# Seven block products in place of eight in six channel groups of a spatial-gating stage, with the values normalized early

## The chip, the cores and the metric

The kernel runs on one core of a Trainium2 chip. A core has five engines that the text names: TensorE (PE) for matrix products, with its weight loads (PEld) shown apart, VectorE (DVE), ScalarE (ACT), GpSimd (POOL) and SyncE (SP), which only issues transfers. Each engine works through its own instructions in order and waits on semaphores for the others. SP and ACT issue the transfers between the chip's memory and the core; sixteen DMA engines carry them. The metric is the device time of one execution in microseconds (us), the median over runs.

## The reference, cut to what matters

One inference step of a two-layer trunk, for 1024 prompt tokens and 64 sample tokens (8 sequences of 8), together 1088 rows of width 1024, in float32. The change touches the even layer:

```python
z = rms_norm(x, norm_g) @ w_in
zq, zk, zv, ga, zu, zvb, gb = split(z)
o_a = rms_norm(diff_attention(q, k, v)) * (1 - lam_init) * silu(ga)
u = gelu(zu)
vb = layer_norm(gelu(zvb), ln_g, ln_b)      # vb of the sample tokens is an output
mixed = chunk_spatial(vb, sp_w, sp_b)       # per group g of 128 channels: w_g (lower triangle, 128x128) times each chunk of 128 tokens, plus sp_b
o_b = u * mixed * silu(gb)
y = x + concat(o_a, o_b) @ w_out
```

`chunk_spatial` works on eight channel groups. For the sample tokens a past of 512 tokens comes from a paged cache of keys and values.

## The kernel before, in words

Tokens stand in columns, in three chunks: 0 and 1 of 384, 2 of 320 (`CH`). The normalized input is held transposed in eight pieces k of 128 channels, split in two numbers: `xh[n]` is its value rounded to a format that PE takes in one pass, `xl[n]` the rest. Weights are split alike (`load_w`): a raw tile arrives by SP, ACT rounds it (hi), DVE or POOL takes the difference (lo). A dense product (`mm3`) is then three matmuls per piece k: hi by `xh`, hi by `xl`, lo by `xh`; eight pieces make 24 matmuls into one PSUM tile.

The stages around the change, in time: attention of the prompt tokens; then the sample attention, which reads 32 pages of keys and 32 of values (`pages`, `vpages`), transposes each key page on PE (`ktp`) and lets ACT copy it back (`kT`, L537); then the spatial stage; then the output projection (`yo`). The sample attention has little work for PE between its waits, so a list `fill` puts other work between its steps, one item after another: first the rest of the gates (`gate_a`: product ga, ACT, DVE, then POOL multiplies the attention rows that ACT has loaded back from `oT_d` as `oTr`, and ACT stores them), then 36 units of value projection (`vb_unit`, product zv, four column blocks by nine row tiles), which store to `vb_d`. `NPRE` gates of 24 stand already in the attention before.

The spatial stage runs over 24 units (group g, chunk n). `b_dense` makes zu and gb, gelu on ACT, the gate by a tanh on ACT, a product on DVE (L743) and one on POOL (u, L744). `b_mix` follows `ML` units later: for each 128 tokens one full float32 matmul of the normalized values by the group's weights (mx, L755), the bias added on DVE (mxs), the product with u on DVE (ob, L766), and a store to `oT_d`. In the first five units `vb_norm` loads the nine row tiles of `vb_d`, gelu on ACT, statistics on DVE, the reciprocal root on POOL (lrv), and two scalings on DVE (L720, L721); `mix_setup` masks and transposes the mixing weights.

Names in tiles carry the group, chunk or piece. Who comes first on an engine is decided when the program is built: instructions go out in the order of a list scheduler, which may interleave neighbouring pieces of the code, and semaphores keep what depends on what.

## Time and profile before

| what | value |
|---|---|
| median of 3 runs | 1791.06 us (1790.74 to 1792.69) |
| profiled execution, its own time | 1789.87 us |
| its span, first to last instruction | 1788.1 us |
| mean granted clock of PE | 0.991 |
| PE busy | 1742.9 us, 97% |
| DVE, ACT, POOL busy | 56%, 42%, 34% |
| spatial stage in the span | 817.9 to about 1028 us |

Times in rows are microseconds of the span, or ns where a mean is given. A timeline row has the start, the length, the engine, the line, the operation and what it writes and reads; "xN" joins N instructions, and a bracket at the end is idle time before it with the one that ended it. A window row gives for each engine the busy time in that stretch.

### The profile page before, as it was taken

To read this page: it belongs to the slowest core of one execution; us is meant where nothing else is said; L and a number is where in the kernel's file an instruction comes from. 1 tells how busy PE (TensorE), PEld (TensorE's weight loads), DVE (VectorE), ACT (ScalarE), POOL (GpSimd) and SP (SyncE) were. 2 spreads that over 40 slices of the span, in tenths; PEclk is the share of its full clock that TensorE was granted. 3 is DMA by queue.
4 is the path that set the end of the run, shared out by engine and by line. 5 is a ranking of instruction groups with operands and counts; after the bars stand their busy time and mean duration, and the time that the engine had idled before them with its cause. 6 is when DMAs were issued, how large, how long until landed. Compare 5 with 4: busy or idle time off the path is not lost.

```text
span 1788.1 us, 31862 instructions
## 1 busy us (share of the span) xinstructions
PE 1742.9 (97%) x11437; PEld 1631.3 (91%) x11437; DVE 1006.3 (56%) x2231; ACT 754.5 (42%) x1934; POOL 605.6 (34%) x881
## 2 busy tenths in 40 slices
PE   8999999999999999999999999999899999998998
PEld 8898999999999888889999999999899999996777
DVE  6988988888892322324833442534265445667442
ACT  5666666665763222223222332423252334345241
POOL 5656655565653221011522100144012223235240
PEclk8999999999999999999999999999999999998999
DMA  7202211220223766747221362433134334438741
GB/s 212 59 20 75 68 42 45 68 67 19 67 71 121 244 218 216 242 142 221 72 77 60 109 188 74 134 94 92 59 121 144 101 119 125 129 116 264 239 127 71
DMA packets 223141, 211.55 MB, mean 118 GB/s; under 512 B 22253, under 2 KB 200982, under 8 KB 222982
## 3 DMA queue, kind: packets, MB, share of 16 engines
q1 hardware_dynamic: 203350, 194.29, 35.1%
q10 hardware_dynamic: 19632, 15.21, 2.8%
q8 instruction: 91, 1.49, 0.4%
q14 instruction: 68, 0.56, 0.1%
HBM read 151.29 MB, written 56.24 MB: 116 GB/s over the span
## 4 chain that ended last, share of the span: by engine, by line
PE 66%; DVE 15%; DMA 6%; ACT 5%; POOL 4%; issue 3%; SPq 0%; ACTq 0%; POOLq 0%; DVEq 0%
PE o L1371 5%; PE yo L148 3%; PE yo L150 3%; PE yo L149 3%; PE vg L148 3%; PE vg L149 3%; PE vg L150 3%; PE zv L148 2%; PE zu L148 2%; PE zv L149 2%; PE zv L150 2%; PE zu L150 2%; PE gb L148 2%; PE zu L149 2%; PE gb L149 2%
## 5 line engine op out<-in xcount | busy, mean ns | idle before, releaser
L409 ACT ACTIVATE p<-s,nm 128x256 f32<-128x256 f32 (+7 forms) x128 | 95.0, 747 | 44.5 <-DVE nm L406 26.1
L396 PE MATMUL s<-ks,qs 128*128 128x512 f32 (+3 forms) x384 | 95.6, 363 | 3.9 <-DVE ks L381 2.2
L92 ACT CAST qs<-qs 64x256 fp32r<-64x256 f32 x128 | 51.7, 404 | 83.5 <-DVE qs L378 77.6
L1118 POOL TENSOR_TENSOR e<-e,k 128x256 f32<-128x256 f32 (+1 forms) x50 | 42.2, 850 | 111.6 <-ACT e L1115 97.6
L396 PEld LDWEIGHTS s<-ks,qs 128*128 128x128 f32 x384 | 64.3, 189 | 14.3 <-ACT qs L92 3.8
L431 PE MATMUL o<-v,at 128*128 128x128 f32 x576 | 75.9, 277 | 1.4 <-ACT at L92 1.4
L136 POOL TENSOR_TENSOR s<-s,mhalf 128x4 f32<-128x4 f32 (+1 forms) x72 | 74.5, 1035 | 5.2
L335 POOL TENSOR_TENSOR sq<-qk 128x256 f32<-128x256 f32 (+1 forms) x72 | 47.8, 664 | 83.1 <-ACT qk L92 82.1
L431 PEld LDWEIGHTS o<-v,at 128*128 128x128 f32 x576 | 70.6, 192 | 4.0 <-ACT at L92 2.4
L834 DVE TENSOR_TENSOR yp<-yp,yo 128x384 f32<-128x384 f32 (+1 forms) x48 | 25.4, 530 | 75.6 <-ACT yp L833 41.7
L404 DVE TENSOR_REDUCE nm<-s 128x1 f32<-128x640 f32 (+3 forms) x64 | 65.2, 1019 | 1.1
L744 POOL TENSOR_TENSOR u<-u,th 128x384 f32<-128x384 f32 (+1 forms) x24 | 28.6, 1192 | 99.8 <-DVE th L743 99.3
L402 DVE TENSOR_TENSOR s<-s,tb 128x256 f32<-128x256 f32 (+1 forms) x128 | 52.5, 412 | 8.9 <-PE s L396 5.8
L415 DVE SCALAR_TENSOR_TENSOR p<-p,fac,p 128x128 f32<-128x128 f32 (+3 forms) x64 | 54.7, 854 | 1.6
L1371 PE MATMUL o<-w1h,oh 128*128 128x512 f32 x128 | 53.0, 414 | 1.2 <-ACT oh L1348 1.2
L92 ACT COPY at<-atp 128x512 f32<-128x512 f32 (+2 forms) x96 | 44.6, 480 | 14.7 <-PE atp L424 14.2
L1371 PE MATMUL o<-w1l,oh 128*128 128x512 f32 x128 | 50.8, 397 | 0.0
L1371 PE MATMUL o<-w1h,ol 128*128 128x512 f32 x128 | 50.3, 407 | 0.0
L743 DVE SCALAR_TENSOR_TENSOR th<-th,gb 128x384 f32<-128x384 f32 (+1 forms) x24 | 12.5, 526 | 65.3 <-ACT th L742 65.3
L424 PE MATMUL atp<-cf,p 128*128 128x128 f32 x288 | 46.7, 273 | 1.7 <-DVE p L415 1.4
L340 POOL TENSOR_TENSOR qk<-qk,s 128x256 f32<-128x256 f32 (+1 forms) x72 | 46.0, 638 | 4.5
L1115 ACT ACTIVATE e<-e 128x512 f32<-128x512 f32 (+1 forms) x50 | 31.1, 623 | 37.4 <-DVE e L1114 33.6
(819 smaller groups left out, 6344.2 us busy)
## 6 DMA issues: line engine op xcount, KB each, us to landing
kp<-in_cache_k SPq DMA_DIRECT2D x32, 512.0 KB
vp<-in_cache_v SPq DMA_DIRECT2D x32, 512.0 KB
or<-oT_d SPq DMA_DIRECT2D x16, 384.0 KB
vb_d<-zs SPq DMA_DIRECT2D x36, 128.0 KB
oT_d<-ob SPq DMA_DIRECT2D x8, 544.0 KB
gt<-g_d SPq DMA_DIRECT2D x34, 128.0 KB
xt<-in_x_prompt SPq DMA_DIRECT2D x8, 512.0 KB
out<-v ACTq DMA_DIRECT2D x64, 64.0 KB
```

The costliest lines, as they stand in the source:

```text
L92: act.activation(o, i_, AF.Copy, scale=scale) if scale is not None else act.copy(o, i_)
L136: pool.tensor_tensor(dst, dst, mhalf[:dst.shape[0], :n], ALU.pow)
L148: pe.matmul(out, lh, rh, start=(s == 0), stop=False)
L149: pe.matmul(out, lh, rl, start=False, stop=False)
L150: pe.matmul(out, ll, rh, start=False, stop=(s == n - 1))
L396: pe.matmul(sc[c][:, k0:k0 + w], qs[:, c, l], kts[h, j][:, c, :w], start=(l == 0), stop=(l == 1))
L402: dve.tensor_tensor(sc[c][:, lo:n], sc[c][:, lo:n], backwards(tb[:, h, 0:n - lo]), ALU.add)
L404: dve.tensor_reduce(nm[:, c:c + 1], sc[c][:, :n], axis=AX.X, op=ALU.max, negate=True)
L409: act.activation(pc[:, :n], sc[c][:, :n], AF.Exp, bias=nm[:, c:c + 1], accum_out=ss[:, c:c + 1])
L415: dve.scalar_tensor_tensor(pt[0][:, :n], pt[1][:, :n], fac, pt[0][:, :n], ALU.mult, ALU.add)
L431: pe.matmul(op[:, :P], at[:, j * P:(j + 1) * P], vts[h, j], start=(j == 0), stop=(j == i))
L1371: pe.matmul(it.mp[:r], lh[:, k, :r], rh[k][:, cs], start=(k == 0 and a == 0), stop=(k == KT - 1 and a == 2))
```

## The change

In groups 2 to 7 (`NCV` = 2) the two projections of chunks 0 and 1 are read as a 2 by 2 block problem: two weight column blocks (zu, gb), two halves of the 1024 input channels, two chunks. The eight products of half by chunk become seven products of sums (Winograd's form): p1 to p7, each of 12 matmuls (four pieces, three parts) of 384 columns. Sums of the input (T1, T2, T4 by `tok_sums`, T3 in place over chunk 1 by `tok_last`) are made once, sums of weight blocks for each group (`load_g`), and seven additions from PSUM put the results together (`b_quad`). Chunk 2 keeps its 48 matmuls of 320 columns.

The normalization goes from the spatial stage into the list `fill`, between the last gates; it stores to a new tensor `vbn_d`, and each group loads its 128 columns (`load_vs`). Gain and bias of the layer norm are taken out of it: the gain enters with mxs, the bias is folded into the mixing bias by two matmuls of 512 columns (wsp) and eight DVE instructions. `fill` now has the 36 value units first and the gates last; `NPRE` goes from 8 to 9. Chunks run in the order 1, 0, 2, and mixing follows one group later.

```diff
-NPRE = 8
+NPRE = 9
...
-ML = 5
+ML = 2
+NCV = 2
+NU = 6
...
+            def vb_norm(i):
+                r = rows(i)
+                vt = pb.tile([P, D], F32, tag="vp", name=f"vbn{i}", bufs=6)
+                nc.sync.dma_start(vt[:r], vb_d[i * P:i * P + r, :])
+                if i == NT - 1:
+                    vx = pb.tile([P, D], F32, tag="vp", name="vx", bufs=6)
+                    nc.sync.dma_start(vx[:r], vb_d[T:, :])
+                    dve.tensor_tensor(vt[:r], vt[:r], vx[:r], ALU.add)
+                act.activation(vt[:r], vt[:r], AF.Gelu)
+                bst = pb.tile([P, 2, 6], F32, tag="bst", name=f"bst{i}", bufs=2)
+                mv = pb.tile([P, 2], F32, tag="mv", name=f"mv{i}", bufs=2)
+                rv = pb.tile([P, 1], F32, tag="lrv", name=f"lrv{i}", bufs=2)
+                for q in range(2):
+                    dve.bn_stats(bst[:r, q, :], vt[:r, q * 512:(q + 1) * 512])
+                dve.bn_aggr(mv[:r], bst[:r].rearrange("p a b -> p (a b)"))
+                rsqrt(rv[:r], mv[:r, 1:2], 1, 1.0)
+                dve.tensor_scalar(vt[:r], vt[:r], mv[:r, 0:1], rv[:r], ALU.subtract, ALU.mult)
...
+                nc.sync.dma_start(vbn_d[i * P:i * P + r, :], vt[:r])
...
+            fill = [lambda c=c, i=i: vb_unit(c, i) for c in range(4) for i in range(NT)]
+            for q, (h, n) in enumerate(du[NPRE:]):
+                fill.append(lambda h=h, n=n: gate_a(h, n, gate_tiles))
+                if 1 < q < NT + 2:
+                    fill.append(lambda i=q - 2: vb_norm(i))
...
+                for hh in range(2):
+                    tp = ps2.tile([P, 512], F32, tag="t", name=f"wsp{hh}", bufs=2)
+                    pe.matmul(tp, ones, wT[:, hh * 4:hh * 4 + 4, :], start=True, stop=True)
+                    for g in range(hh * 4, hh * 4 + 4):
+                        dve.scalar_tensor_tensor(sbc[:, g, :], tp[:, g % 4 * P:(g % 4 + 1) * P], lnc[1][:, g:g + 1], sbc[:, g, :],
+                                                 ALU.mult, ALU.add)
...
+            def put_split(t, k, src):
+                act.copy(t[0][:, k, :], src)
+                dve.tensor_tensor(t[1][:, k, :], src, f32(t[0][:, k, :]), ALU.subtract)
+
+            def tok_diff(k, name):
+                a, c = temp(f"{name}a{k}"), temp(f"{name}c{k}")
+                pool.tensor_tensor(a, f32(xl[1][:, k + 4, :]), f32(xl[1][:, k, :]), ALU.subtract)
+                dve.tensor_tensor(c, f32(xh[1][:, k + 4, :]), f32(xh[1][:, k, :]), ALU.subtract)
+                dve.tensor_tensor(c, c, a, ALU.add)
+                return c
+
+            def tok_sums():
+                for m in (1, 2, 4):
+                    tx[m] = [pb.tile([P, 4, XW], F32R, name=f"t{m}{q}") for q in "hl"]
+                for k in range(4):
+                    a, c = temp(f"ta{k}"), temp(f"tc{k}")
+                    pool.tensor_tensor(a, f32(xl[1][:, k, :]), f32(xl[0][:, k, :]), ALU.subtract)
+                    dve.tensor_tensor(c, f32(xh[1][:, k, :]), f32(xh[0][:, k, :]), ALU.subtract)
+                    dve.tensor_tensor(c, c, a, ALU.add)
+                    put_split(tx[1], k, c)
+                    c = tok_diff(k, "td")
+                    dve.tensor_tensor(c, c, f32(xh[0][:, k, :]), ALU.add)
+                    dve.tensor_tensor(c, c, f32(xl[0][:, k, :]), ALU.add)
+                    put_split(tx[2], k, c)
+                    e = temp(f"te{k}")
+                    dve.tensor_tensor(e, f32(xh[0][:, k + 4, :]), c, ALU.subtract)
+                    dve.tensor_tensor(e, e, f32(xl[0][:, k + 4, :]), ALU.add)
+                    put_split(tx[4], k, e)
+
+            def tok_last():
+                tx[3] = xh[1], xl[1]
+                for k in range(4):
+                    put_split(tx[3], k, tok_diff(k, "tf"))
...
+            def load_g(g):
...
+                gs = []
+                for k in range(4):
+                    gt = pb.tile([P, 8, P], F32, tag="G", name=f"G{g}_{k}", bufs=4)
+                    for x in range(2):
+                        nc.sync.dma_start(gt[:, 3 * x:3 * x + 2, :],
+                                          ap_of(w_in0[0], k * P * n + (4 + 2 * x) * D + g * P, [[n, P], [4 * P * n, 2], [1, P]]))
+                    dve.tensor_tensor(gt[:, 6], gt[:, 3], gt[:, 4], ALU.add)
+                    dve.tensor_tensor(gt[:, 5], gt[:, 0], gt[:, 3], ALU.subtract)
+                    dve.tensor_tensor(gt[:, 2], gt[:, 6], gt[:, 0], ALU.subtract)
+                    dve.tensor_tensor(gt[:, 7], gt[:, 1], gt[:, 2], ALU.subtract)
+                    gs.append(gt)
+                blk = Wg_[g] = [[None] * 4 for _ in range(8)]
+                for a, e in ((0, 3), (3, 6), (6, 8)):
+                    for k in range(4):
+                        hi = pw.tile([P, e - a, P], F32R, tag="wh", name=f"gh{g}_{a}_{k}", bufs=9)
+                        lo = pw.tile([P, e - a, P], F32R, tag="wl", name=f"gl{g}_{a}_{k}", bufs=9)
+                        act.copy(hi, gs[k][:, a:e, :])
+                        (pool if a == 3 else dve).tensor_tensor(lo, gs[k][:, a:e, :], f32(hi), ALU.subtract)
+                        for q in range(a, e):
+                            blk[q][k] = hi[:, q - a, :], lo[:, q - a, :]
...
+            def b_quad(g):
...
+                act.copy(pa_, prod("p1_", A11, xb(0, 0)))
+                add(pb_, pa_, prod("p6_", S2, tb_(2)))
+                add(u[0], pa_, prod("p2_", A12, xb(0, 4)))
+                act.activation(u[0], u[0], AF.Gelu)
+                act.activation(u[2][:, :w2], prod("zu2_", A11 + A12, xb(2, 0) + xb(2, 4), w2), AF.Gelu)
+                add(pa_, pb_, prod("p7_", S3, tb_(3)))
+                p5 = prod("p5_", S1, tb_(1))
+                add(pd_, pa_, p5)
+                add(pb_, pb_, p5)
+                bf = prod("gb2_", A21 + A22, xb(2, 0) + xb(2, 4), w2)
+                add(u[1], pb_, prod("p3_", S4, xb(1, 4)))
+                act.activation(u[1], u[1], AF.Gelu)
+                add(pa_, pa_, prod("p4_", A22, tb_(4)))
+                for n, gv in ((2, bf), (1, pd_), (0, pa_)):
+                    th = tile_("th", f"th{n}_", 2)
+                    gated(u[n], g, n, th, gv)
...
+            order = [(g, n) for g in range(NCV) for n in (1, 0, 2)]
+            for s, (g, n) in enumerate(order):
+                us[g, n] = b_dense(g, n)
+                if s == 0:
+                    load_b(1)
+                    tok_sums()
                 if s == 1:
                     mix_setup()
-                for i in range(2 * s, min(2 * s + 2, NT)):
-                    vb_norm(i)
-                n = 0
-                while s >= ML and mi < min(s, len(units)) and n < 2:
-                    b_mix(*units[mi], us.pop(mi))
-                    mi += 1
-                    n += 1
+                if (g, n) == (NCV - 1, 1):
+                    tok_last()
+                    load_g(NCV)
+                if g and n == 1:
+                    load_vs(g)
+                if g:
+                    b_mix(g - 1, n, us.pop((g - 1, n)))
+            for g in range(NCV, KT + 1):
+                if g < KT:
+                    us.update({(g, n): t for n, t in enumerate(b_quad(g))})
+                    load_vs(g)
+                    load_g(g + 1)
+                for n in (1, 0, 2):
+                    b_mix(g - 1, n, us.pop((g - 1, n)))
 
     lY = ctx.enter_context(ExitStack())
     pY = lY.enter_context(tc.tile_pool(name="pY", bufs=1, side="right", reuse_waits="tile"))
```

The order on ACT ahead of the first copy of transposed keys (kT, sample 0), before. `oT_d<-oTr` is a gate's store, `oTr<-oT_d` a gate's load, g the gate's activation.

```order
L550 DMA vn_8379<-vsm 8x1024
L255 DMA oT_d<-oTr_2_7898 128x256
L250 ACTIVATE g_3_0_7932<-ga_0_7930 128x384
L248 DMA oTr_1_8006<-oT_d 128x384
L255 DMA oT_d<-oTr_0_7931 128x384
L250 ACTIVATE g_3_1_8007<-ga_1_8005 128x384
L248 DMA oTr_2_8061<-oT_d 128x256
L537 COPY kT_1_7981<-ktp_0_1_7988 128x4x128
```

And after; zs is the copy of a value unit from PSUM.

```order
L253 ACTIVATE g_2_2_7853<-ga_2_7851 128x320
L94 ACTIVATE oT_7541<-otp_6_7884,sg 128x128
L94 ACTIVATE oT_7541<-otp_7_7887,sg 128x128
L258 DMA oT_d<-oTr_2_7852 128x256
L554 DMA vn_8422<-vsm 8x1024
L251 DMA oTr_0_10273<-oT_d 128x384
L624 COPY zs_1_8014<-zv_1_7989 128x256
L251 DMA oTr_1_10415<-oT_d 128x384
L624 COPY zs_3_8118<-zv_3_8093 128x256
L541 COPY kT_1_8018<-ktp_0_1_8025 128x4x128
```

Two gate stores and two gate loads ahead of kT have become one store and two loads, with copies of value units between the loads and kT.

The order on POOL from the start of the spatial stage, before. lrv is the reciprocal root of the normalization, u the gated product.

```order
L684 AFFINE_SELECT wn<-wn 128x128 x8
L135 TENSOR_SCALAR lrv_11540<-mv_11539 128x1
L136 TENSOR_TENSOR lrv_11540<-lrv_11540,mhalf 128x1
L744 TENSOR_TENSOR u_0_11482<-u_0_11482,th_0_11484 128x384
L135 TENSOR_SCALAR lrv_11552<-mv_11551 128x1
L136 TENSOR_TENSOR lrv_11552<-lrv_11552,mhalf 128x1
L744 TENSOR_TENSOR u_1_11610<-u_1_11610,th_1_11612 128x384
L135 TENSOR_SCALAR lrv_11653<-mv_11652 128x1
L136 TENSOR_TENSOR lrv_11653<-lrv_11653,mhalf 128x1
L744 TENSOR_TENSOR u_2_11723<-u_2_11723,th_2_11725 128x320
```

And after. ta, tda are differences of `xl` for T1 and T2, g2s and oTr the last gate.

```order
L256 COPY g2s<-g_7_2_11430 128x64
L257 TENSOR_TENSOR oTr_2_11429<-oTr_2_11429,g_7_2_11430 128x256
L819 TENSOR_TENSOR ta_11665<-xl_102,xl_101 128x384
L809 TENSOR_TENSOR tda_11672<-xl_102 128x384
L771 TENSOR_TENSOR u_1_11605<-u_1_11605,th_1_11607 128x384
L725 AFFINE_SELECT wn<-wn 128x128 x8
L819 TENSOR_TENSOR ta_11686<-xl_102,xl_101 128x384
L809 TENSOR_TENSOR tda_11693<-xl_102 128x384
L771 TENSOR_TENSOR u_0_11799<-u_0_11799,th_0_11801 128x384
L819 TENSOR_TENSOR ta_11707<-xl_102,xl_101 128x384
L771 TENSOR_TENSOR u_2_11900<-u_2_11900,th_2_11902 128x320
L809 TENSOR_TENSOR tda_11714<-xl_102 128x384
```

The reciprocal roots are gone from here, and differences of 128x384 stand between the u, in the same queue.

The order on SP late in the sample attention, before. kp and vp are pages of keys and values (ISA sets their address), `vb_d<-zs` the store of a value unit.

```order
L525 ISA
L525 DMA vp_2_10537<-in_cache_v 128x1024
L518 ISA
L518 DMA kp_1_10548<-in_cache_k 128x1024
L525 ISA
L525 DMA vp_3_10657<-in_cache_v 128x1024
L518 ISA
L518 DMA kp_2_10668<-in_cache_k 128x1024
L525 ISA
L525 DMA vp_0_10719<-in_cache_v 128x1024
L621 DMA vb_d<-zs_2_10584 128x256
```

And after. vbn is a row tile of values, loaded from `vb_d` and stored normalized to `vbn_d`.

```order
L529 ISA
L529 DMA vp_3_10744<-in_cache_v 128x1024
L634 DMA vbn_10798<-vb_d 128x1024
L522 ISA
L522 DMA kp_2_10755<-in_cache_k 128x1024
L180 DMA wb0r_11510<-in_w_in 128x2x128
L180 DMA wb0r_11516<-in_w_in 128x2x128
L648 DMA vbn_d<-vbn_10661 128x1024
L180 DMA wb0r_11522<-in_w_in 128x2x128
L648 DMA vbn_d<-vbn_10798 128x1024
L529 ISA
L529 DMA vp_0_10823<-in_cache_v 128x1024
```

Loads and stores of 512 KB for the normalization now stand between the pages.

## Rows read from the trace of the kernel before

**Rows 1.** The page, parts 1 and 2: busy time and tenths of PE.
```profile
PE 1742.9 (97%) x11437; PEld 1631.3 (91%) x11437; DVE 1006.3 (56%) x2231; ACT 754.5 (42%) x1934; POOL 605.6 (34%) x881
PE   8999999999999999999999999999899999998998
```

**Rows 2.** Stretches: length, busy PE, PEld, DVE, ACT, POOL, granted clock, DMA share, GB/s.
```profile
580.00:600.00 20.00, 16.33 (x91) 16.01 (x90) 4.55 (x8) 4.21 (x9) 3.89 (x5) 0.83 0.68 218
...
740.00:760.00 20.00, 20.00 (x180) 18.07 (x179) 7.20 (x16) 6.70 (x18) 3.08 (x4) 1.00 0.85 286
...
820.00:840.00 20.00, 20.00 (x125) 19.93 (x124) 8.28 (x24) 8.94 (x17) 2.76 (x10) 1.00 0.92 313
840.00:860.00 20.00, 20.00 (x123) 19.68 (x123) 20.00 (x42) 9.46 (x17) 8.02 (x11) 1.00 0.45 119
860.00:880.00 20.00, 20.00 (x125) 20.00 (x124) 20.00 (x31) 5.46 (x13) 15.91 (x10) 1.00 0.23 65
```

**Rows 3.** Waits of PE from 560 to 1040 us: total, times, longest.
```profile
PE ktp L536 <- ACT kT L537: 3.7, 1, 3.7
PE ktp L536 <- DMA kp<-in_cache_k: 0.7, 1, 0.7
```

**Rows 4.** Timeline of PE, first group of the spatial stage: start, length, instruction.
```profile
817.86 0.34 PE L148 MATMUL zu<-xh,wb0h 128*128 128x384 f32 x1
...
824.05 0.33 PE L148 MATMUL zu<-xh,wb0h 128*128 128x384 f32 x1
...
826.13 0.33 PE L149 MATMUL gb<-xl,wb0h 128*128 128x384 f32 x1
```

**Rows 5.** Timeline of PE: mixing matmuls, and one page's key transposes.
```profile
914.16 0.83 PE L755 MATMUL mx<-wT,vb 128*128 128x128 f32 x6
...
596.01 1.04 PE L536 MATMUL ktp<-cf,kp 128*128 128x128 f32 x8
```

**Rows 6.** Timeline of ACT and its queue around the long wait.
```profile
582.48 0.37 ACTq L255 DMA_DIRECT2D oT_d<-oTr  x1
...
587.98 0.33 ACTq L248 DMA_DIRECT2D oTr<-oT_d  x1
588.35 0.59 ACT L537 COPY kT<-ktp 128x512 f32<-128x512 f32 x1 [4.91 <-DMA oT_d<-oTr]
```

**Rows 7.** Stretches of 2 us after that wait, columns as in rows 2.
```profile
588.00:590.00 2.00, 1.01 (x5) 1.02 (x6) 0.62 (x2) 1.41 (x3) 0.17 (x1) 0.55 0.67 215
590.00:592.00 2.00, 2.00 (x8) 2.00 (x8) 1.43 (x3) 1.23 (x3) 0.84 (x1) 0.50 0.49 112
...
594.00:596.00 2.00, 2.00 (x10) 1.98 (x9) 0.00 (x0) 0.00 (x0) 0.00 (x0) 0.75 0.93 315
```

**Rows 8.** Lines by form in the spatial stage: count, busy us, mean ns.
```profile
L759 DVE TENSOR_TENSOR mxs<-mx,sbc 128x384 f32<-128x384 f32 x16 | 8.7, 549 | 2.0 <-PE mx L755 2.0
L763 DVE TENSOR_TENSOR mxs<-mx,sbc 128x64 f32<-128x64 f32 x7 | 1.5, 214 | 0.0
L740 ACT ACTIVATE u<-zu 128x384 f32<-128x384 f32 x16 | 7.8, 490 | 46.3 <-PE zu L150 46.3
```

**Rows 9.** Timeline of DVE: products of u and mxs.
```profile
877.57 0.54 DVE L766 SCALAR_TENSOR_TENSOR ob<-u,mxs 128x384 f32<-128x384 f32 x1
...
906.75 0.88 DVE L766 SCALAR_TENSOR_TENSOR ob<-u,mxs 128x320 f32<-128x320 f32 x1
...
916.06 0.95 DVE L766 SCALAR_TENSOR_TENSOR ob<-u,mxs 128x384 f32<-128x384 f32 x1
```

**Rows 10.** Timeline of POOL beside them.
```profile
867.85 5.85 POOL L744 TENSOR_TENSOR u<-u,th 128x384 f32<-128x384 f32 x2
...
906.25 1.02 POOL L744 TENSOR_TENSOR u<-u,th 128x384 f32<-128x384 f32 x1 [7.00 <-DVE th L743]
...
915.58 1.02 POOL L744 TENSOR_TENSOR u<-u,th 128x384 f32<-128x384 f32 x1 [8.31 <-DVE th L743]
```

**Rows 11.** The page, part 6: page loads by SP.
```profile
vp<-in_cache_v SPq DMA_DIRECT2D x32, 512.0 KB
```

More of the change, by code (lines that the diff above doesn't have):

```diff
@@ L623, in vb_unit @@
                     load_vb(c + 1)
-            fill = [lambda h=h, n=n: gate_a(h, n, gate_tiles) for h, n in du[NPRE:]]
-            fill += [lambda c=c, i=i: vb_unit(c, i) for c in range(4) for i in range(NT)]
+                    if c == 3:
+                        load_gate(NPRE // len(CH))
+            def vb_norm(i):
[16 more added lines that the diff above has]
+                nc.sync.dma_start(vbn_d[i * P:i * P + r, :], vt[:r])
+                if i == NT - 1:
+                    lnt = [pb.tile([P, D], F32, tag="vp", name=f"ln{q}", bufs=6) for q in range(2)]
+                    vs = pb.tile([P, D], F32, tag="vp", name="vsout", bufs=6)
+                    nc.sync.dma_start(lnt[0][:r], ln_v_g.broadcast_to([r, D]))
+                    nc.sync.dma_start(lnt[1][:r], ln_v_b.broadcast_to([r, D]))
+                    pool.tensor_tensor(vs[:r], vt[:r], lnt[0][:r], ALU.mult)
+                    pool.tensor_tensor(vs[:r], vs[:r], lnt[1][:r], ALU.add)
+                    nc.sync.dma_start(vb_sample.rearrange("e b t d -> (e b t) d"), vs[:r])
@@ L748, in b_mix @@
                 c0, cw = CH[n]
[L749 removed]
+                if g not in obs:
                     obs[g] = pb.tile([P, T], F32, tag="ob", name=f"ob{g}", bufs=1)
@@ new lines, in gated, with xb, tb_, tile_ @@
+            def gated(u, g, n, th, gv):
+                cw = CH[n][1]
+                act.activation(th[:, :cw], gv[:, :cw], AF.Tanh, scale=0.5)
+                dve.scalar_tensor_tensor(th[:, :cw], th[:, :cw], 1.0, gv[:, :cw], ALU.add, ALU.mult)
+                pool.tensor_tensor(u[:, :cw], u[:, :cw], th[:, :cw], ALU.mult)
+            def b_quad(g):
+                A11, A12, S2, A21, A22, S3, S1, S4 = Wg_[g]
+                def xb(n, k0):
+                    return [(xh[n][:, k, :], xl[n][:, k, :]) for k in range(k0, k0 + 4)]
+                def tb_(m):
+                    return [(tx[m][0][:, k, :], tx[m][1][:, k, :]) for k in range(4)]
+                def tile_(tag, name, bufs):
+                    return pb.tile([P, XW], F32, tag=tag, name=f"{name}{g}", bufs=bufs)
+                u = [tile_("u", f"u{n}_", NU) for n in range(3)]
+                th = [None] * 3
+                pa_ = pw.tile([P, XW], F32, tag="wr", name=f"pa{g}", bufs=4)
+                pb_ = pw.tile([P, XW], F32, tag="wr", name=f"pb{g}", bufs=4)
+                w2 = CH[2][1]
+                pd_ = temp(f"pd{g}")
+                def prod(name, ws, xs_, w=XW):
+                    t = ps2.tile([P, 512], F32, tag="mm", name=f"{name}{g}", bufs=6)
+                    mm3(t[:, :w], [(wh, wl, rh, rl) for (wh, wl), (rh, rl) in zip(ws, xs_)])
+                    return t[:, :w]
+                def add(out, a, c):
+                    dve.tensor_tensor(out, a, c, ALU.add)
+                act.copy(pa_, prod("p1_", A11, xb(0, 0)))
[14 more added lines that the diff above has]
+                    gated(u[n], g, n, th, gv)
+                return u
@@ L770, in hybrid_step @@
             load_b(0)
[L771 removed]
+            load_vs(0)
             us = {}
[L773 to L778 removed]
+            order = [(g, n) for g in range(NCV) for n in (1, 0, 2)]
[4 more added lines that the diff above has]
+                    tok_sums()
```

77 lines of the change are left out of this document (32 added, 45 removed).

## The prediction

> **What bounds the kernel now.** The page's parts 1 and 2 come first: TensorE (PE) is busy 97% of the span, and its row of tenths is at 9 nearly everywhere [rows 1]. So a change pays by what it takes from PE's own stream or from PE's few waits. Then come the 20 us stretches around the spatial stage, which begins when the first of its matmuls starts, at 817.86 us [rows 4]: PE shows 20.00 of 20 from 820 to 880, at full granted clock, even where VectorE (DVE) is at 20.00 of 20 as well; only 580 to 600 stands out, with 16.33 and a clock of 0.83 [rows 2]. The list of PE's waits from 560 to 1040 says why: one wait of 3.7 us, for the copy of transposed keys on ScalarE (ACT), and under 2 us of others [rows 3]. Two places therefore matter: PE's stream in the stage, and that one wait.
>
> **Products removed.** In before every group issues 96 matmuls of 384 columns (two projections, two chunks, eight row blocks of weights, three products of the split numbers); after, groups 2 to 7 issue seven blocks of 12, which is 84. 6 x 12 = 72 go. The thirteen starts from 824.05 to 826.13 are 12 steps in 2.08 us, 0.173 us each [rows 4]; 320 columns take 0.144 in proportion. 72 x 0.173 = **-12.5 us**, all on PE and so on the path. The weight loads of the removed matmuls lie beside matmuls and give nothing.
>
> **Products added.** Two full float32 matmuls of 512 columns (wsp). The nearest row is mx, three float32 matmuls of 128 columns in six records: 0.83 us with a last record of 0.28, so 0.11 per record, 0.22 per matmul [rows 5]; four times the columns, 0.89 each, **+1.8**. If columns cost as in the 384 rows, it is 2 x 0.23 = 0.5; I take 1.8, since the mx row has the same number type.
>
> **The wait at 585 us.** In before the copy kT stands on ACT behind a gate load that waits until an earlier gate store has landed: the store is issued at 582.48, the next load at 587.98, kT runs at 588.35, 4.91 us idle [rows 6]. PE stops for 3.67 [rows 3], and the granted clock then reads 0.55, 0.50, again 0.50 and 0.75 in four stretches of 2 us [rows 7]: at the lower level, 1.2 GHz, after an idle time at 2.4. The missing shares, 0.45 + 0.50 + 0.50 + 0.25 = 1.7 of 2 us, cost 3.4 us. After, the order shows two gate loads ahead of that kT, each separated from the store it needs by several copies and by units of value projection (zv) on PE, and no further gate store. I let the whole wait go: **-7.0** (bounds -7.0 and 0: a late store could hold kT there too).
>
> **Token sums.** DVE gets 44 instructions of 128x384 (T1, T2, T4), 12 more for T3, and per group 16 additions of 128x128, 8 roundings and 7 additions from PSUM; GpSimd (POOL) gets 12 subtractions of 128x384. Normalization leaves the stage: in before it fills DVE from 840 to 880, but PE was full there [rows 2], so its going alone saves nothing. PE's dates, counted from the stage's start by the steps above: group 0 with its extras ends at 26.5 us, group 1 at 52.3, then p1, p6, p2 and zu2, p7 at 62.1; its last quarter, which reads the last part of T3, at 63.6. DVE: the third instruction in order waits for the first tanh, after two blocks of 24 matmuls and two ACT instructions of 0.49 [rows 8], at 9 us. Then up to that part of T3: 54 token instructions at 0.55 = 29.7; 20 additions of 128x128 at 0.3 (between 0.21 for 64 and 0.55 for 384 columns [rows 8]) = 6.0; 12 weight roundings, 5.3; gates, mixing and output of two groups, 6.6; copies and folds of the mixing set-up, 4.5: 52 us, done at 61. That is 2.6 us in hand, if nothing stretches.
>
> Something stretches. A 128x384 product of u and mxs takes DVE 0.54 alone (at 877.57), 0.95 when POOL's u is running; that DVE instruction started at 916.06, POOL ended at 916.60, and DVE at 917.01. At 906.75 one with only 320 columns took 0.88, again ending behind POOL's u [rows 9, 10]. Instructions with an input from PSUM are not stretched: mxs has a mean of 0.549 over all 16 [rows 8]. Where DVE was full, POOL paid: two u took 5.85 us at 867.85, against 1.02 each later [rows 10]. From 9 to 61 us POOL has 19 such instructions (token differences, u, roundings). At 0.45 each on DVE that is 8.6, less the 2.6 in hand: 6.0 late; a part falls where DVE waits anyway. I take **+5**, in several pieces, with nothing for the clock. Lower bound 0; upper bound in the rival below.
>
> The Trainium skill (SBUF — State Buffer, "Who interferes with whom") says that a VectorE instruction with two SBUF inputs and a GpSimd instruction that reads SBUF exclude each other for the whole instruction. The two rows with the stretched DVE agree (0.95 against 0.54); in the stretch from 867.85 it is POOL that is long. By the rule alone the two engines' times add, which is the slower rival's sum.
>
> **Later groups.** Per group PE has 84 x 0.173 + 48 x 0.144 + 2.1 of mixing = 23.5 us. DVE has 4.8 of additions, 3.9 of roundings, 3.9 from PSUM, 1.6 of gates, 3.3 of mixing and output: 17.5. POOL has four roundings and three u at about 1.02: 7.1. There is room, but the weight pieces of the next group can be rounded only when the present group's products have freed their slots, so a POOL rounding that comes late reaches PE. 0.5 per group, **+3** (0 to 6 x 1.1, the excess of 17.5 + 7.1 over 23.5).
>
> **The end of the attention stage.** The fill is reversed: 36 value units first, gates with nine normalizations last. SP, which issues in order, now has the stores of normalized values ahead of V pages, and each store waits for gelu, statistics and scaling. By the order, from the second page of sample 6 to the last of sample 7 PE issues 120 gate matmuls of 384 columns, 48 of 320 and thirteen times four key transposes (0.52, half of the eight in [rows 5]): 20.8 + 6.9 + 6.8, with some 8 us of scores and values, an estimate, 42. In that time SP moves 24 transfers of 512 KB (11 pages [rows 11], the rest normalization of the same size), 12.6 MB, 300 GB/s; before reached 286 and 313 in 20 us stretches with PE at 20.00 [rows 2]. At 313 all is in time, at 286 it is 2 us late: **+1.5** (0 to 14: two waits like the one at 585 us). The stage after gets its rows from DVE and POOL later: **+0.5** (0 to 2).
>
> **Sum.** -12.5 + 1.8 - 7.0 + 5 + 3 + 1.5 + 0.5 = -7.7. The profiled execution took 1789.87 us (span 1788.1), which gives 1782.2; the median of the runs is 1.2 higher, 1791.06, so **1783**.
>
> **Rivals.**
> 1. Everything stays covered: 1791.06 - 12.5 + 1.8 - 7.0 = 1773.4. For it: PE at 20.00 beside a full DVE [rows 2]; against it: the stretched rows [rows 9], and a count with only 2.6 us in hand.
> 2. The wait at 585 us stays or only moves, while the 10 us of new waits come: 1783 + 7 = 1790, no change. For it: gate loads are still ahead of kT on ACT, and a store took 5.5 us to land [rows 6]; against it: more work stands between store and load.
> 3. Slower: DVE and POOL take turns through the token sums. Place: from the tanh to T3; price: 19 POOL instructions of 1.02 put wholly on DVE's 52 us, so T3 at 61 + 19.4 = 80.4, 16.8 after PE wants it, plus 3.4 of low clock as after 585 us; then 1.1 in each of six groups. -17.7 + 20.2 + 6.6 + 2 = +11.1: 1802. It decides against the change once the wait at T3 exceeds 17.7 less the rest's 5, about 13 us. For it: DVE ends with POOL [rows 9]; against it: POOL, not DVE, paid in the full stretch [rows 10].
> 4. Slower as well: SP's stores hold the pages, and PE stops four times in the last 44 us, each at the 3.67 + 3.4 of rows 3 and 7: -7.7 + 28 = 1811; with two stops 1797. For it: 300 GB/s due; against it: PE's waits for pages in before come to 0.7 us [rows 3].
>
> That the change does not do what it says I exclude: the order of PE has the 72 fewer.
>
> **Chances.** Forecast 0.42 (own range 1778 to 1788), rival 1 0.26, rival 2 0.13, rival 3 0.12, rival 4 0.07. A measurement of this kernel can tell about 0.2%, 3.6 us. Faster: 0.41 + 0.26 + 0.03 = 0.70; rival 2 puts 0.08 within 0.2% and 0.02 above, rival 4 with few stops and the forecast's edge 0.03 within: same 0.11; slower 0.19. The range leaves out the best part of rival 1 and the worst of rivals 3 and 4: 1773 to 1798.
>
> **What would show it.** In the profile after: 72 fewer matmuls of 384 columns in the stage; no wait of PE for kT near 585 us and a granted clock of 1.00 there; PE's waits for T3 (xh, xl) or for the first rounded weights of group 2, 3 to 7 us; u on POOL at 1.5 to 3 us during the token sums. I am wrong if PE idles over 10 us at the token sums, if it waits for V pages at the end of the attention stage, or if the stage is shorter by the full 10.7 with no new wait.

## The result, and the profile after

The changed kernel is slower by 0.6%: 1802.39 us median of five runs (1800.57 to 1804.66) against 1791.06 for the kernel before on the same chip, a ratio of 1.0061 (95% interval 1.0045 to 1.0077). The forecast was 1783, the range ended at 1798. The profiled execution took 1800.57 (span 1798.8).

Parts 1 and 2 of the page after answer to [rows 1]. TensorE's (PE's) records fall by 68: 72 products gone, two wsp matmuls in four records added. Its share is still 97%, and its busy time falls by 5.1 us while the span grows by 10.7.

```profile
PE 1737.8 (97%) x11369; PEld 1620.2 (90%) x11369; DVE 1100.6 (61%) x2444; ACT 780.8 (43%) x1984; POOL 639.2 (36%) x899
PE   8999999999999999998999999999899999998999
```

The stretches of after, with the columns of [rows 2]; the spatial stage now begins at 830.49, and the two stretches of 6 us lie around PE's longest wait:

```profile
580.00:600.00 20.00, 20.00 (x173) 20.00 (x172) 4.04 (x7) 3.09 (x6) 0.00 (x0) 1.00 0.79 256
...
800.00:820.00 20.00, 14.57 (x107) 12.52 (x106) 11.42 (x22) 9.45 (x20) 5.43 (x11) 0.92 0.80 238
820.00:840.00 20.00, 17.66 (x88) 17.40 (x87) 10.11 (x12) 2.64 (x6) 11.21 (x10) 0.83 0.65 170
840.00:860.00 20.00, 20.00 (x122) 19.00 (x121) 17.55 (x47) 5.50 (x13) 10.04 (x13) 1.00 0.62 169
860.00:880.00 20.00, 20.00 (x124) 19.68 (x123) 18.08 (x45) 6.49 (x15) 8.42 (x5) 1.00 0.05 14
880.00:900.00 20.00, 16.97 (x87) 15.51 (x86) 19.79 (x29) 6.71 (x16) 12.18 (x10) 0.83 0.21 69
...
812.00:818.00 6.00, 0.78 (x4) 0.54 (x4) 3.34 (x6) 2.64 (x4) 0.53 (x2) 0.89 1.04 269
818.00:824.00 6.00, 6.00 (x22) 6.00 (x21) 4.02 (x6) 0.94 (x4) 4.02 (x7) 0.54 0.86 260
```

The hole at 580 has closed. Three new ones stand at the end of the sample attention (800 to 824), at the stage's first group (830) and at 886: PE idle first, then a clock near one half, the 1.2 GHz level. PE's waits from 560 to 1040 name them, in the form of [rows 3] (total, times, longest):

```profile
PE ga L151 <- DVE g L254: 5.2, 1, 5.2
PE ktp L540 <- DMA kp<-in_cache_k: 4.2, 3, 1.9
PE zu L151 <- DVE g L254: 2.3, 1, 2.3
PE p L151 <- ACT gh L859: 1.7, 1, 1.7
PE p L153 <- DVE gl L860: 1.3, 1, 1.3
PE zv L151 <- ACT oT L94: 1.0, 1, 1.0
```

Where the time went is read from PE's own dates in two parts. **Sample attention** here runs from the first 320-column matmul of the third gate (568.66 before, 568.32 after) to the first zu; **stage and output** from there to the first vg matmul behind the output projection (1237.06, 1248.36). The two dates of after, in PE's timeline (the column of [rows 4]):

```profile
568.32 0.39 PE L151 MATMUL ga<-xh,wg2h 128*128 128x320 f32 x1
...
830.49 0.69 PE L151 MATMUL zu<-xh,wb0h 128*128 128x384 f32 x1 [2.34 <-DVE g L254]
```

The parts outside gave back about 1.

| | before | forecast | after |
|---|---|---|---|
| sample attention | 249.2 | 243.7 (-7.0, +1.5) | 262.2 |
| stage and output | 419.2 | 417.0 (-12.5 +1.8 +5 +3 +0.5) | 417.9 |

Stage and output came out within 1 us. The sample attention is 18.5 us longer than forecast, and that is nearly the whole miss. Between the two dates PE idles 13.8 us (4.4 before) and loses 3.0 to half clock (3.0 before); the other 3.6 us of the 13.0 that it grew lie in steps between matmuls that the trace shows as busy, and no run says why.

The 5.2 us wait followed back. A gate's last step on VectorE (DVE) that reads its product is g, L254; it frees the PSUM tile that the next gate needs. DVE's timeline has it behind two instructions of the normalization, and these behind loads:

```profile
813.18 1.29 DVE L644 BATCH_NORM_STATS2 bst<-vbn 128x6 f32<-128x512 f32 x2 [1.49 <-ACT vbn L639]
...
815.79 1.22 DVE L638 TENSOR_TENSOR vbn<-vbn,vx 64x1024 f32<-64x1024 f32 x1 [1.00 <-DMA vx<-vb_d]
816.93 0.47 DVE L254 SCALAR_TENSOR_TENSOR g<-g,ga 128x320 f32<-128x320 f32 x1
```

SP's timeline shows those loads (L634, L637), the stores of normalized rows (L648) and the last page (L529):

```profile
783.03 0.33 SPq L529 DMA_DIRECT2D vp<-in_cache_v  x1
...
795.46 0.34 SPq L634 DMA_DIRECT2D vbn<-vb_d  x1
795.92 0.35 SPq L648 DMA_DIRECT2D vbn_d<-vbn  x1
801.05 0.32 SPq L634 DMA_DIRECT2D vbn<-vb_d  x1
805.57 0.32 SPq L648 DMA_DIRECT2D vbn_d<-vbn  x1
808.30 0.88 SPq L634 DMA_DIRECT2D vbn<-vb_d  x2
809.29 0.53 SPq L637 DMA_DIRECT2D vx<-vb_d  x1
```

Four of the nine row tiles are loaded after the last page, and three times from 785 to 812 SP stands in front of L634 until a store `vbn_d<-vbn` has landed, 7.9 us in all. In the form of [rows 3], for SP's queue:

```profile
SPq L634 <- DMA vbn_d<-vbn: 7.9, 3, 4.7
```

The row tiles, vx, the gains and 32 pages of values all draw on one ring of six slots (tiles with the same tag, here "vp", take turns in `bufs` slots). A row tile gives its slot back only after load, gelu, statistics, scaling and store, so pages and rows hold each other up.

### The profile page after: what moved, and what is told of

Same layout as the page of the kernel before. It is cut to its first block, busy times and chain, and to the rows that moved or that the text cites. A ratio compares the mean times of both kernels' runs of the same rounds, so it can differ in the third digit from the quotient of the medians.

```text
span 1798.8 us, 32098 instructions
## 1 busy us (share of the span) xinstructions
PE 1737.8 (97%) x11369; PEld 1620.2 (90%) x11369; DVE 1100.6 (61%) x2444; ACT 780.8 (43%) x1984; POOL 639.2 (36%) x899
## 4 chain that ended last, share of the span: by engine, by line
PE 42%; DVE 4%; DMA 4%; issue 2%; ACT 2%; POOL 1%; SPq 0%; ACTq 0%; DVEq 0%; POOLq 0%
PE o L1523 5%; PE yo L151 3%; PE yo L153 3%; PE yo L152 3%; PE vg L151 3%; PE vg L152 3%; PE vg L153 3%; PE p L151 1%; PE p L152 1%; PE p L153 1%; PE qk L153 1%; PE qk L151 1%; PE qk L152 1%; PE lp L1289 1%; PE gb L152 1%
## 5 line engine op out<-in xcount | busy, mean ns | idle before, releaser
L868 POOL TENSOR_TENSOR u<-u,th 128x384 f32<-128x384 f32 (+1 forms) x18 | 24.2, 1345 | 90.6 <-DVE th L867 88.7
L94 ACT COPY at<-atp 128x512 f32<-128x512 f32 (+2 forms) x96 | 44.7, 481 | 14.8 <-PE atp L428 14.2
L382 DVE SCALAR_TENSOR_TENSOR qs<-qkt,qg,qs 64x128 fp32r<-64x128 f32 x128 | 44.6, 348 | 3.6
```

Of the source, the lines that this page charges most:

```text
L94: act.activation(o, i_, AF.Copy, scale=scale) if scale is not None else act.copy(o, i_)
```

## The experiments

Ratios are to the kernel before on the same chip, with 95% interval; the two parts are in us, from the same two dates, in the one profiled execution of each kernel. A second profile of before gives 247.6 and 419.6. After and the four versions that leave its sample attention as it is (no_block_products, three_plain_groups, differences_on_dve, no_token_sums) take 262.2 to 267.5 there, so a few us between two profiles prove nothing by themselves. Where an expectation gives the sample attention of a changed version as 245.9 or 249, it counts from the end of that gate, 3.6 us later than the table.

| kernel | ratio | sample attention | stage and output |
|---|---|---|---|
| after | 1.0061 [1.0045, 1.0077] | 262.2 | 417.9 |
| no_second_half | 1.0084 [1.0062, 1.0106] | 263.1 | 419.3 |
| no_norm_in_tail | 0.9982 [0.9971, 0.9994] | 249.5 | 416.3 |
| no_block_products | 1.0115 [1.0097, 1.0133] | 263.0 | 427.2 |
| three_plain_groups | 1.0083 [1.0068, 1.0098] | 267.5 | 419.5 |
| reversed_list_alone | 0.9993 [0.9981, 1.0005] | 247.4 | 418.8 |
| four_gate_tiles | 1.0070 [1.0056, 1.0084] | 253.6 | 426.2 |
| differences_on_dve | 1.0049 [1.0033, 1.0065] | 263.9 | 411.9 |
| no_token_sums | 1.0128 [1.0109, 1.0146] | 266.2 | 422.1 |
| own_slots | 1.0002 [0.9987, 1.0017] | 252.9 | 416.8 |
| norm_two_gates_earlier | 1.0061 [1.0044, 1.0077] | 265.3 | 418.3 |
| earlier_and_dve | 1.0035 [1.0018, 1.0051] | 263.2 | 410.9 |
| own_slots_and_dve | 0.9980 [0.9969, 0.9991] | 253.1 | 411.9 |
| own_slots_plain_groups | 1.0073 [1.0051, 1.0095] | 252.9 | 428.3 |
| own_slots_all_and_dve | 0.9992 [0.9978, 1.0006] | 256.2 | 413.1 |
| own_slots_dve_four_tiles | 0.9993 [0.9979, 1.0007] | 251.4 | 413.6 |

Letters in the expectations name the reasons in dispute at the time, each told in the words beside it.

**no_second_half**: the second half of the last row tile is not loaded and added.
```diff
-                    nc.sync.dma_start(vx[:r], vb_d[T:, :])
-                    dve.tensor_tensor(vt[:r], vt[:r], vx[:r], ALU.add)
```


> This kernel leaves out the addition of the second half (vx) to the sample rows of the values, one load and one DVE instruction at the end of the sample attention; the rest is the changed kernel, 1802.4 us. Theory A (the normalization's instructions stand in DVE's in-order queue ahead of the gate products that free PE's result tiles, and the one that waits for vx holds the last gates): PE's wait of 5.2 us for g and the 3.4 us of low clock behind it go or fall under 2 us together, 1794 to 1797. Theory B (too many bytes at the end of the sample attention, so that whatever is loaded there is late): another load takes the place of vx, the wait for g stays at 4 us or more, 1801 to 1803.


PE's wait for g stays, 5.1 us. DVE now waits for the gelu (2.36), and the gelu for a row load (2.75) that SP issued at 805.86. First DVE's row, then ScalarE's (ACT):
```profile
811.38 1.28 DVE L640 BATCH_NORM_STATS2 bst<-vbn 128x6 f32<-128x512 f32 x2 [2.36 <-ACT vbn L635]
```
```profile
810.29 1.06 ACT L635 ACTIVATE vbn<-vbn 128x1024 f32<-128x1024 f32 x1 [2.75 <-DMA vbn<-vb_d]
```
The load of vx was only the last of several late ones; my first theory fell.

**no_norm_in_tail**: the nine normalizations are left out of the list, the stage loads from vb_d.
```diff
-                if 1 < q < NT + 2:
-                    fill.append(lambda i=q - 2: vb_norm(i))
...
```


> This kernel leaves the normalization out (the mixing reads the raw values, the sample output too); the reversed list of other work and the block products stay. Theory A and theory B: every new wait at the end of the sample attention is the normalization's, so the spatial stage begins about 18 us earlier, near 811 us, with PE's waits for g and most of the 4.2 us for key pages gone, 1783 to 1786. Rival D (the list in reverse, gates last, is itself late, through the gates' loads and stores on ACT): the stage begins at 822 us or later, 1794 or more.


The sample attention falls by 12.7 us and the wait for g at the gates is gone. The normalization among the last gates costs that, and neither the turned list nor the block products do. Whether it is its work or the place of its loads, this version can't tell.

**no_block_products**: all eight groups plain, normalization where after has it.
```diff
-NCV = 2
+NCV = 8
...
```


> All eight groups by eight products, without sums of tokens or of weight blocks; the early normalization and the reversed list stay. The end of the sample attention is as in the changed kernel (stage begins near 830.5). Theory C (sums of tokens and weights made late by DVE and POOL give back about 8 of the 12.5 us): the stage and what follows are 12.5 longer by products and about 8 to 9 shorter by waits and low clock, so 1802.4 + 4 = 1805 to 1808. Rival (the waits at group 2 are carried in from the late start of the stage, and cost nothing of the block products' own): 1812 to 1815.


Stage and output lengthen by 9.3 us, and the sample attention stays as it was (263.0): the block products pay, and the loss in the sample attention has nothing to do with them.

**three_plain_groups**: block products one group later.
```diff
-NCV = 2
+NCV = 3
```


> NCV = 3: groups 0 to 2 by eight products, so the sums have one group (about 25 us) more. Theory C (a deadline missed by DVE): PE's waits of 3.0 us at the first block products and the 3.3 us of low clock behind them go, for 2.1 us of products: 1797 to 1799.5. Rival (the wait is a chain of slots and casts on ACT that comes with the first converted group wherever it stands): the wait stays, 1803 to 1806.


One more group in which the token sums may run changes little in the stage. The wait moved to the weights of plain group 2, near 891:
```profile
PE zu L151 <- ACT wb2h L182: 2.0, 1, 2.0
PE zu L153 <- DVE wb2l L183: 1.3, 1, 1.3
```
So it is not one date (T3) that DVE misses; whatever is next in DVE's and ACT's queues at that time comes late. The sample attention, where nothing was edited, has 5 us more; the profiled execution is the slowest of the five (1808.94, median 1804.03), so this need not be an effect of the edit.

**reversed_list_alone**: the kernel before, its list turned (value units first, then gates).
```diff
-NPRE = 8
+NPRE = 9
-            fill = [lambda h=h, n=n: gate_a(h, n, gate_tiles) for h, n in du[NPRE:]]
-            fill += [lambda c=c, i=i: vb_unit(c, i) for c in range(4) for i in range(NT)]
+            fill = [lambda c=c, i=i: vb_unit(c, i) for c in range(4) for i in range(NT)]
+            fill += [lambda h=h, n=n: gate_a(h, n, gate_tiles) for h, n in du[NPRE:]]
...
```


> The kernel before with nothing but the list turned round (value units first, gates last, nine gates ahead). With the normalization left out, the sample attention of the changed kernel took 245.9 us against 250.2 of before, so the turned list alone should be 3 to 5 us faster than before (ratio 0.997 to 0.9985), the 585 us wait gone and no wait of PE for g over 1.5 us. If the turned list needs the emptier DVE that the left-out normalization gave the stage, the gain is under 1 us.


PE is at 20.00 from 580 to 600 and the sample attention takes 247.4, 1.8 us less than in one profile of before and 0.2 less than in the other. PE idles 2.7 us there and loses nothing to half clock, 4.7 less than the 7.4 in the first profile of before; its busy steps take 2.9 longer, which is not explained. The whole time can't be told from no change. The expectation set 245.9 behind the third gate against 250.2 ahead of it; between the same dates, no_norm_in_tail has 249.5 and before 249.2.

**four_gate_tiles**: half of the last gates use the two PSUM tiles of the key transposes.
```diff
-                return (psb.tile([P, 512], F32, tag="mm", name=f"ga{h}_{n}", bufs=2),
+                return (psb.tile([P, 512], F32, tag="kt" if h > 5 and (h + n) % 2 else "mm", name=f"ga{h}_{n}", bufs=2),
```


> The changed kernel with the last six gates taking turns between the two result tiles of the value units and the two of the key transposes, four in place of two; DVE's order and every transfer are as they were. Theory A (PE waits because DVE comes late to the gate products that free the tiles): PE runs two gates on, the 5.2 us wait and its 3.4 us of low clock go, the stage begins 5 to 8 us earlier, ratio to before 1.001 to 1.004 against 1.006. Theory B (bytes: loads late whatever waits for them): PE stands as long at another place there, 1.005 to 1.007.


The wait for g goes and the sample attention is 8.6 us shorter, but the stage starts before its inputs are there and gives 8.3 back:
```profile
PE wtp L731 <- POOL wn L725: 2.3, 3, 1.8
PE p L153 <- DVE gl L860: 2.1, 2, 1.3
PE zu L153 <- DVE wb0l L183: 1.8, 2, 1.5
```
Taking away the last wait of a late chain moves the lateness on.

**differences_on_dve**: the token differences leave GpSimd (POOL).
```diff
-                pool.tensor_tensor(a, f32(xl[1][:, k + 4, :]), f32(xl[1][:, k, :]), ALU.subtract)
+                dve.tensor_tensor(a, f32(xl[1][:, k + 4, :]), f32(xl[1][:, k, :]), ALU.subtract)
-                    pool.tensor_tensor(a, f32(xl[1][:, k, :]), f32(xl[0][:, k, :]), ALU.subtract)
+                    dve.tensor_tensor(a, f32(xl[1][:, k, :]), f32(xl[0][:, k, :]), ALU.subtract)
```


> The twelve token differences that POOL makes are made by DVE. Theory C (DVE instructions with two inputs in the core's memory are stretched from 0.55 to 1.3 us beside one of POOL's): DVE gets 6.6 us more and loses about 10 us of stretch; the waits at the first block products (3.0 and 3.3 of low clock) shrink to 1 us or less, ratio 1.002 to 1.005. Rival E (DVE has too much work there, whoever stands beside it): 6 us more of it makes the waits 5 to 9 us, 1.007 to 1.011.


DVE gets 12 instructions more, and stage and output become 6.0 us shorter. DVE by form from 835 to 905 (count, busy us, mean ns), first after, then this kernel:
```profile
L860 DVE TENSOR_TENSOR gl<-G,gh 128x384 fp32r<-128x384 f32 x5 | 5.1, 1037 | 0.0
L810 DVE TENSOR_TENSOR tfc<-xh 128x384 f32<-128x384 f32 x4 | 4.0, 988 | 0.0
L825 DVE TENSOR_TENSOR tdc<-tdc,xl 128x384 f32<-128x384 f32 x4 | 3.7, 928 | 0.1
```
```profile
L860 DVE TENSOR_TENSOR gl<-G,gh 128x384 fp32r<-128x384 f32 x5 | 3.5, 708 | 0.0
L825 DVE TENSOR_TENSOR tdc<-tdc,xl 128x384 f32<-128x384 f32 x4 | 2.2, 550 | 0.1
L810 DVE TENSOR_TENSOR tfc<-xh 128x384 f32<-128x384 f32 x4 | 2.2, 546 | 0.0
```
These three lines alone give 4.9 us back. The ratios show less than the profiles: 2.1 us against after, whose interval overlaps, and 4.7 and 3.9 in the two pairs below (earlier_and_dve, own_slots_and_dve), all three the same way. PE's waits among the products fall to 0.8, 0.3 and 0.2 us, and no half clock follows them.

**no_token_sums**: the block products use plain x in place of T1 to T4.
```diff
-                    tx[m] = [pb.tile([P, 4, XW], F32R, name=f"t{m}{q}") for q in "hl"]
+                    tx[m] = xh[0], xl[0]
```


> This kernel leaves the sums of tokens out (the seven products take plain tokens); the sums of weights, the seven products and the early normalization stay. If the 56 DVE instructions of the sums make the weights of group 2 late, PE's waits of 3.0 us there and the low clock of 3.3 go, stage and output projection are 7 to 9 us shorter, ratio 1.001 to 1.0025. If the weight sums are late by themselves (slots, casts), a wait of 2 us or more stays at group 2 and the ratio is 1.004 to 1.006.


The spatial stage by itself falls from 204.2 to 197.4 us, somewhat further than with the differences on DVE (198.6), but the output projection grows from 213.6 to 224.8: seven waits there for its ACT and DVE copies (oh, ol; 7.0 us), and 4.7 us lost to half clock. The total misses every expectation; why the output's copies come so late is not settled.

**before_again**: the kernel before, unedited, for one more profile.


> The kernel before, profiled once more. If the wait at 585 us (3.7 us for the copy of keys, with 3.4 us of low clock) belongs to every execution, it is there again, and the turned list is worth 7 us by the profile. If it comes and goes with the landing of one gate store, PE's wait is under 1.5 us here and the span is 3 to 6 us shorter than the 1788.1 of the first profile; that would also say why the turned list alone gave 0.999 by the medians and not 0.996.


It took 1787.39. The wait for kT is there, at 2.2 us instead of 3.7, without half clock behind it, and another of 1.2 us comes at 613:
```profile
PE ktp L536 <- ACT kT L537: 3.4, 2, 2.2
```
That hole is not the same in each execution.

**own_slots**: the row tiles get two slots of their own, the pages keep four.
```diff
-                vp = pb.tile([P, D], F32, tag="vp", name=f"vp{b}_{g}", bufs=6)
+                vp = pb.tile([P, D], F32, tag="vp", name=f"vp{b}_{g}", bufs=4)
-                vt = pb.tile([P, D], F32, tag="vp", name=f"vbn{i}", bufs=6)
+                vt = pb.tile([P, D], F32, tag="vbn", name=f"vbn{i}", bufs=2)
...
```


> The changed kernel with the six shared tiles of the V pages divided: four for V pages, two for the row tiles of the normalization, so that a load of values no longer waits for PE to be done with a V page. Theory F (shared slots and SP's order make the last loads late): the last row tiles are loaded 5 us or more sooner, PE's wait for g falls under 2 us, the sample attention is 4 to 8 us shorter, ratio 1.001 to 1.004. Theory B (bytes): the loads are as late, the wait for g is 4 to 5 us, 1.005 to 1.008. If V pages then come late instead, PE waits at the products with V.


9.3 us come back in the sample attention, and 10.5 in the whole by the ratios, with the same bytes and no slot more than after has. SP's last row load is now 36 us earlier and ahead of the last pages; only vx still waits for a page's slot:
```profile
772.66 0.53 SPq L634 DMA_DIRECT2D vbn<-vb_d  x1
...
785.38 1.47 SPq L529 DMA_DIRECT2D vp<-in_cache_v  x3
809.63 0.47 SPq L637 DMA_DIRECT2D vx<-vb_d  x1
```
Row loads still stand behind stores (three times, 6.8 us from 700 to 820), but earlier. The edit changes SP's order along with the slots; the two were not tried apart.

PE's waits from 566 to the stage, with none left in front of a gate:
```profile
PE ktp L540 <- DMA kp<-in_cache_k: 2.6, 3, 1.4
PE zu L151 <- DVE g L254: 2.3, 1, 2.3
PE sot L602 <- DVE son L594: 1.2, 1, 1.2
PE zv L151 <- ACT oT L94: 1.0, 1, 1.0
```

**norm_two_gates_earlier** and **earlier_and_dve**: each normalization two gates sooner in the list, slots shared as in after; the second has the differences on DVE as well.
```diff
-                if 1 < q < NT + 2:
-                    fill.append(lambda i=q - 2: vb_norm(i))
+                if q < NT:
+                    fill.append(lambda i=q: vb_norm(i))
```


> The nine normalizations follow the first nine of the last gates in the list, in place of the third to the eleventh; nothing else. Theory A with F (a chain SP, ACT, DVE, POOL that ends too late for the last gates and for what the stage needs first): the chain ends 8 us or more earlier, the wait for g goes, and as rounded weights and mixing weights are earlier too nothing moves on into the stage: ratio 1.000 to 1.003. Theory B (bytes): the same bytes in a shorter time come no earlier, 1.005 to 1.007.

> Both: normalizations two gates earlier, and the token differences on DVE, which alone gave 1.0049 against 1.0061. If the two costs stand apart, the ratio is that of norm_two_gates_earlier less 0.001 to 0.003: 0.997 to 1.001. If the earlier normalization only lets DVE's backlog begin earlier, the differences on DVE bring nothing more.


The wait for g falls to 3.3 us in both and the key pages' waits rise (from 4.2 to 6.9 and 5.2): the sample attention stays as long (265.3 and 263.2). An earlier place in the list doesn't help while the slots are shared. The gain on DVE repeats (418.3 to 410.9).

**own_slots_and_dve**: own_slots and differences_on_dve together.
```diff
+                vt = pb.tile([P, D], F32, tag="vbn", name=f"vbn{i}", bufs=2)
...
+                dve.tensor_tensor(a, f32(xl[1][:, k + 4, :]), f32(xl[1][:, k, :]), ALU.subtract)
```


> Own tiles for the normalization (alone 1.0002) and the token differences on DVE (alone 1.0049 against 1.0061 of the change). If the two costs stand apart, 0.996 to 0.999, faster than both kernels: sample attention near 249 us, stage and output projection near 411. If the stage's waits were fed by the late attention, the second edit adds nothing: 1.000 to 1.002.


0.998: the one version that does the whole work and beats both kernels, 1784.55 against 1789.19. The gain is 0.1 to 0.3%. PE from 840 to 900 is full again:
```profile
840.00:860.00 20.00, 20.00 (x118) 18.72 (x117) 19.73 (x61) 6.77 (x16) 3.40 (x3) 1.00 0.14 41
860.00:880.00 20.00, 20.00 (x128) 19.81 (x127) 19.90 (x35) 7.40 (x18) 11.24 (x7) 1.00 0.22 70
880.00:900.00 20.00, 20.00 (x128) 19.81 (x127) 19.61 (x49) 8.99 (x21) 6.48 (x5) 1.00 0.15 42
```

**own_slots_plain_groups**: own_slots without block products.
```diff
-NCV = 2
+NCV = 8
...
```


> Own tiles for the normalization, all eight groups by eight products, no sums. Against own_slots (1.0002) it gives what the block products are worth in the changed kernel as it stands: if their 12.5 us are mostly given back by DVE and POOL, 1.001 to 1.003 (2 to 5 us slower); if they were worth their full 11 us once the attention's end is mended, 1.006.


The block products, with what their sums cost, are worth 428.3 - 416.8 = 11.5 us. Without them the new arrangement costs 9.1 us against before's 419.2: 4.7 of half clock (3.0 behind the last gate's wait, 1.7 in the output projection), 2.3 more idle time, 0.9 for wsp; 1.2 are not assigned to a cause.

**own_slots_all_and_dve** and **own_slots_dve_four_tiles**: own_slots_and_dve, in the first with vx, gains and vsout in other tags too, in the second with the edit of four_gate_tiles.
```diff
-                    vx = pb.tile([P, D], F32, tag="vp", name="vx", bufs=4)
+                    vx = pb.tile([P, D], F32, tag="kp", name="vx", bufs=2)
...
```


> As own_slots_and_dve, and the four extra tiles of the last row tile (second half, gain, bias, output) use the tiles of the key pages and of the normalization, so that no load there waits for V pages; in own_slots SP stood 9.7 us for PE's products with V. If this holds the rest of the loss, the sample attention falls from 249 to 244 to 246 us, as with the normalization left out, ratio 0.993 to 0.997; if not, it is that of own_slots_and_dve within 0.001.

> own_slots_and_dve (0.998) with four result tiles for the last six gates. With the normalization's chain on time, the waits of 1.1 and 2.4 us before the stage and 1.7 us of low clock behind them may go without coming back: 0.995 to 0.997. If the stage's first rounded weights and mixing weights are late themselves, as in four_gate_tiles, it is 0.998 within 0.001, with waits for wb0 or wn in the stage.


Neither gains more. In the first a gate waits again (3.0); in the second other waits come (sot 2.2, t2l 1.3).

## Why the prediction was wrong

- **Failed: "The end of the attention stage", +1.5 (0 to 14).** Against the turned list alone (247.4) the sample attention of after takes 14.8 us more, 13.3 above the term; leaving the normalization out gives 12.7 of it, own slots 9.3. The step summed bytes against a rate (300 GB/s due, 286 to 313 seen) and looked for waits on pages. Bytes over rate did not decide: 238 GB/s move from 800 to 820, and own slots win 9.3 us with the same bytes. While PE waits, 269 GB/s keep the DMA engines busy all the time (share 1.04), so the late loads also shared them; what that adds was not measured. What the step left out is the ring of six slots that the added row tiles share with the pages, and that a load into such a slot waits for the store from it to land. Nor did it follow the late load through DVE's queue to g and the gate's PSUM tile. The first could be read before, as `tag="vp"` stands in the diff; the second stands in the order on DVE, L638 ahead of g, which the prediction did not look at. The upper end of 14 comes close in size, but it was two waits for pages. The 5.5 us that own slots leave against the turned list have no single cause shown.
- **Mis-sized: the wait at 585 us, -7.0.** The wait went, as forecast; the size was one execution's. The second profile of before has 2.2 us there and no half clock, and the turned list alone is worth 0.2 to 1.8. That is another 5 to 7 us of the miss.
- **Products removed, -12.5.** The 72 are gone, and the count by steps holds. No run prices them alone: the differences of 9.3 (no_block_products) and 11.5 (own_slots_plain_groups) include the cost of the sums, where -12.5 + 5 + 3 = -4.5 was forecast, and also the half clock and waits that the plain versions have and before has not.
- **Products added, +1.8.** 0.91 measured for both wsp matmuls; the other value in the text (0.5) was closer.
- **Token sums +5, later groups +3.** Near in size, and the mechanism is seen: beyond the steps of [rows 4] the 384-column products of the stage take 8.2 us more than in before. 1.6 of it is half clock in the first group, behind the last gate's wait, so not theirs; the rest is waits and half clock among the products of groups 2 to 7. Taking POOL's differences off gives 6.0 back in one profile and 2 to 5 by the ratios. The sign on POOL came half: u took 1.14 us with 384 columns and 2.34 with 320, where 1.5 to 3 was forecast. The place differs: PE waited for rounded weights (gh, gl) of group 2 at 886, the alternative that the text named, and three_plain_groups shows that no single deadline is at work. Nothing was allowed for the clock; half clock is about half of it.
- **Rivals.** Rival 3's 1802 is the time measured, for another reason: its wait at T3, 16.8 us, came to 3.0 us at the weights. A number that fits is no proof of a mechanism. Rival 4 had the place (SP's stores at the end of the attention stage) but pages as the victims; key pages do cost 4.2 us, and the larger part went through the gates. At 0.07 it was priced from PE's page waits in before, where the added loads did not exist. Rival 1 is excluded by the waits at 886, and rival 2 by the full stretch from 580 to 600.

## What to carry to other kernels

When a step with loads and stores is moved into a stage that streams, list the buffers it takes and who else takes turns in that ring, and follow a late load down each in-order queue to the tile that PE needs; bytes over rate is only a lower bound. Give a moved stream slots of its own, even out of the same total. Keep SBUF-to-SBUF work off POOL while DVE is the engine that is late, and size a removed wait by more than one execution.

## What the hardware showed that I had not expected

DVE waits for a running POOL instruction and then does its own work: in these two pairs of after, each DVE instruction ends 0.40 to 0.41 us after POOL's, as at 916 in [rows 9, 10]. First DVE's, then POOL's timeline:
```profile
872.95 1.37 DVE L793 SCALAR_TENSOR_TENSOR ob<-u,mxs 128x384 f32<-128x384 f32 x1
874.25 1.36 DVE L825 TENSOR_TENSOR tdc<-tdc,xl 128x384 f32<-128x384 f32 x1
```
```profile
872.65 1.27 POOL L771 TENSOR_TENSOR u<-u,th 128x384 f32<-128x384 f32 x1 [1.66 <-DVE th L770]
873.87 1.33 POOL L819 TENSOR_TENSOR ta<-xl,xl 128x384 f32<-128x384 f32 x1
```
So 0.55 us becomes 1.37. The Trainium skill (SBUF — State Buffer, "Who interferes with whom") says that a VectorE instruction with two inputs in SBUF and a GpSimd instruction that reads SBUF exclude each other for a whole instruction. These rows agree, and so do three instructions on POOL at 889.00 that take 3.64 us while DVE beside them takes 1.37 for one and 2.65 for two.

Columns of a float32 matmul are not paid in proportion: four records of wsp (512 columns) take 0.91 us, 0.23 each, against 0.11 for mx (128 columns, [rows 5]).

Moving gelu among softmax steps also makes ScalarE reload its tables: five loads of 1.28 us from 560 to 1040, one in before. No run here prices them apart, but own_slots has seven and the shorter sample attention.
